# A hybrid convolution block on one core: every pool of 4 KB tiles moved to a multiple of 4 KB in SBUF

## The chip, the core and the metric

The kernel runs on one core of a Trainium2 chip. TensorE (PE, with its weight loads listed as PEld) multiplies, VectorE (DVE) and ScalarE (ACT) work elementwise, GpSimd (POOL) only writes a few constants here, and SyncE (SP) issues nearly all loads and stores. The metric is the device time of one execution in microseconds (us). SBUF is the on-chip memory: 128 partitions, and a tile has the same byte address in each of them. "Remainder" below means a tile's byte address within a partition modulo 4096.

## What is computed

One layer over 256 tokens and 4096 channels, all in float32. The reference, cut to what matters:

```python
c_act = jax.nn.silu(c)
mod = c_act @ w_ada[l] + b_ada[l]                       # 4096 x 12288
shift, scale, gate = jnp.split(mod, 3, axis=-1)
h = _rmsnorm(x, norm_g[l]) * (1.0 + scale[:, None, :]) + shift[:, None, :]
proj = jnp.einsum("bsd,de->bse", h, w_in[l])            # 4096 x 14336
a_b, a_c, a_x, a_z, b_v, b_g, b_z = jnp.split(proj, SPLITS, axis=-1)
y_a = a_b * _causal_depthwise_conv(a_c * a_x, conv_a_w[l]) * jax.nn.silu(a_z)
u = _causal_depthwise_conv(b_v * jax.nn.sigmoid(b_g), conv_b_w[l]) + conv_b_b[l]   # width 31
y_b = jax.nn.silu(_layernorm(u, ln_b_g[l], ln_b_b[l])) * jax.nn.silu(b_z)
x = x + gate[:, None, :] * jnp.einsum("bse,ed->bsd", jnp.concatenate([y_a, y_b], -1), w_out[l])
return _rmsnorm(x, final_g)
```

## The kernel before

**Products.** Each float32 operand is split into a high part (rounded to the format that TensorE multiplies in one pass) and a low rest. `load_w` loads a weight tile of two rows of 128 and 512 columns (512 KB, 4 KB in each partition) into a raw tile `w_r`, ScalarE rounds it to `w_h` (L137), VectorE subtracts to get `w_l` (L138). `products` (L150 to L152) then issues 12 matmuls for the tile: for each of the two rows and the two halves of the tokens, activation-high times `w_h`, activation-high times `w_l`, activation-low times `w_h`. The 512 columns that stream through TensorE (the moving operand, 2 KB in each partition) are always `w_h` or `w_l`; the 128 columns of the activations (`hT` or `yT`, 512 bytes) are loaded as weights before each matmul. There are 576 weight tiles, so 6,912 such matmuls.

**Stages.** The first 448 weight tiles are those of `w_in` (tiles `ps`), taken in six blocks over the 4096 input channels; between them VectorE forms the modulation by dot products over 256 loaded tiles of `w_mod` (L186), and later over 128 tiles of `w_gate`. The width-31 convolution (L347 on ScalarE, L348 on VectorE) is spread over the steps from the last block on. Then come 64 weight tiles of `w_out` for the first half of the channels (tiles `pa`) and 64 for the second half (`pb`). A step is one weight tile; a queue sorted by step numbers says which other work is issued in which step.

**The last 96 matmuls.** The last column tile of `w_out` is done in two passes over the same eight weight tiles: 48 matmuls for the first half of the tokens, then 48 for the second. For the first five of these eight weight tiles (`HOLD = 5`, `keep` in `load_w`) `w_h` and `w_l` lie in the pool `big`, not in the pool `split`. So in each pass 30 matmuls stream out of `big` and then 18 out of `split`; their weights (`yT`) lie in `big` in all of them.

**Pools.** SBUF is filled from address 0 in the order of the pools, and every tile starts at a multiple of 32 bytes. `big` holds 33 tiles of 4 KB (`hT`, `yT`, `acc`, `cv`, `xs` and so on), `cbc` one tile of 16 KB (`cB`, read by L186), `part` four tiles of 16 bytes (running sums of L186), `raws` seven tiles of 4 KB (every raw load), `split` three `w_h` and three `w_l` of 4 KB. The first 16 KB are scratch for DMAs whose descriptors GpSimd writes; this kernel issues none of those. The pools begin at:

| pool | before | remainder | after | remainder |
|---|---|---|---|---|
| `big` | 22,752 | 2,272 | 12,288 | 0 |
| `cbc` | 157,920 | 2,272 | 147,456 | 0 |
| `raws` | 174,432 | 2,400 | 163,840 | 0 |
| `split` | 203,104 | 2,400 | 192,512 | 0 |
| end of `split` | 227,680 | | 217,088 | |

Of the kernel before, what the change touches and what calls it, by code (L numbers as in the profile page):

```python
# [1 line left out]

# [10 lines left out]
F32 = mybir.dt.float32  # L13
# [4 lines left out]
P = 128  # L18
# [65 lines left out]
def decoder_block(ctx: ExitStack, tc: tile.TileContext, x, c, w_mod, w_gate, w_in, w_out, xt, pk, final_g, out):  # L84
    nc = tc.nc
    const = ctx.enter_context(tc.tile_pool(name="const", bufs=1))
    big = ctx.enter_context(tc.tile_pool(name="big", bufs=33))
    cbc = ctx.enter_context(tc.tile_pool(name="cbc", bufs=1))
    part = ctx.enter_context(tc.tile_pool(name="part", bufs=4))
    dram = ctx.enter_context(tc.tile_pool(name="dram", bufs=1, space=bass.MemoryType.DRAM))  # L90
    raws = ctx.enter_context(tc.tile_pool(name="raws", bufs=7))
    split = ctx.enter_context(tc.tile_pool(name="split", bufs=3))
# [6 lines left out]
    def rawt(name, shape=(P, 2, 512)):  # L99
        return raws.tile(list(shape), F32, tag="r", name=name)  # L100
# [59 lines left out]
    modT = const.tile([P, 64], F32, name="modT")  # L160
    gscT = const.tile([P, KT], F32, name="gscT")
    gateT = const.tile([P, KT], F32, name="gateT")
    cB = cbc.tile([P, D], F32, name="cB")
    hT = {}

# [10 lines left out]
    def ada_steps(name, srcs, bias, dst):  # L176

        state = {}

        def step(q):  # L180
            raw = rawt(f"{name}_{q}", (P, ROW))
            nc.sync.dma_start(raw, srcs[q])
            if q == 0:
                state["part"] = part.tile([P, 4], F32, tag="part", name=f"part{name}")
            p = state["part"]
            nc.vector.tensor_tensor_reduce(out=raw, in0=raw, in1=cB[:, q * ROW:(q + 1) * ROW], scale=1.0, scalar=p[:, q - 1:q] if q else bias, op0=ALU.mult, op1=ALU.add, accum_out=dst if q == D // ROW - 1 else p[:, q:q + 1])  # L186

        return [lambda q=q: step(q) for q in range(D // ROW)]
# [431 lines left out]
```

## Time and profile before

| what | value |
|---|---|
| time, median of 3 runs | 1765.87 us (1765.5 to 1768.59) |
| the profiled execution | 1770.85 us, of which its span is 1769.1 us |
| busy: PE, DVE, ACT | 1675.3, 1423.0, 1163.1 us |
| TensorE clock granted over the span | 0.984 of full speed |
| moved by DMA | 524.51 MB, 296 GB/s over the span |

The span runs from the first to the last instruction. Busy times overlap, and matmuls are pipelined: one is on record for about 0.4 us though the next starts some 0.23 us after it. So the pace of TensorE is read from the starts of its matmuls, not from their lengths.

### The profile page before, as it was taken

Reading aid. Unit: us, or ns where it says so; the run is one execution under the profiler, and the core shown is the slowest. Engines: PE = TensorE matmul, PEld = TensorE weight load, DVE = VectorE, ACT = ScalarE, POOL = GpSimd, SP = SyncE. Lnnn points to the kernel's source line nnn. Section 1 sums busy time; section 2 is a strip of 40 time slices with the busy share of each in tenths; the row PEclk is TensorE's granted clock in tenths of the full one; section 3 lists DMA queues with packets and bytes.
Section 4 is the critical chain, followed back from the end, with each engine's and each line's share of the span. In section 5 each row is a group of like instructions: output and inputs, shape, how many; then the busy total and the mean of one; then the engine's idle time right before and its main releaser. Section 6 shows DMA issues by size and latency. Waiting matters only on the chain.

```text
span 1769.1 us, 20848 instructions
## 1 busy us (share of the span) xinstructions
PE 1675.3 (95%) x7073; PEld 1328.7 (75%) x7073; DVE 1423.0 (80%) x1707; ACT 1163.1 (66%) x1558; POOL 1.0 (0%) x8
## 2 busy tenths in 40 slices
PE   4799999999999999999999999989888999999997
PEld 1577788888888888888887787766666777778885
DVE  6877777777777777777776889999999999976665
ACT  4555966566666555565655699898898777464453
POOL 0000000000000000000000000000000000000000
PEclk9899999999999999999999999999999999999998
DMA  8998999999989999999998998868787999678663
GB/s 322 318 367 317 315 325 325 323 320 318 321 312 338 318 313 313 318 330 313 315 320 301 330 317 284 288 225 274 266 266 257 320 313 317 221 272 313 193 199 142
DMA packets 146771, 524.51 MB, mean 296 GB/s; under 512 B 16196, under 2 KB 16228, under 8 KB 146664
## 3 DMA queue, kind: packets, MB, share of 16 engines
q1 hardware_dynamic: 146520, 522.81, 85.3%
q8 instruction: 55, 0.90, 0.2%
q14 instruction: 52, 0.43, 0.1%
q10 hardware_dynamic: 144, 0.37, 0.1%
HBM read 518.91 MB, written 4.21 MB: 296 GB/s over the span
## 4 chain that ended last, share of the span: by engine, by line
PE 66%; DVE 17%; issue 9%; ACT 4%; DMA 4%; DVEq 0%; ACTq 0%
PE ps L151 18%; PE ps L152 17%; PE ps L150 17%; DVE w_l L138 5%; DVE cv L348 5%; DVE gate L186 3%; PE pb L152 3%; PE pb L150 3%; PE pb L151 3%; DMA mod<-in_w_mod 2%; ACT w_h L137 2%; DMA gate<-in_w_gate 1%; ACT pr L347 1%; DVE mod L186 1%; PE pa L151 1%
## 5 line engine op out<-in xcount | busy, mean ns | idle before, releaser
L138 DVE TENSOR_TENSOR w_l<-w_r,w_h 128x1024 fp32r<-128x1024 f32 x576 | 700.5, 1222 | 257.6 <-ACT w_h L137 252.0
L137 ACT CAST w_h<-w_r 128x1024 fp32r<-128x1024 f32 x576 | 598.9, 1045 | 279.0 <-PE ps L152 148.4
L151 PE MATMUL ps<-w_l,hT 128*128 128x512 f32 x1792 | 717.0, 400 | 26.4 <-DVE w_l L138 26.4
L150 PE MATMUL ps<-w_h,hT 128*128 128x512 f32 x1792 | 711.8, 398 | 25.9 <-ACT hT L156 17.8
L152 PE MATMUL ps<-w_h,hT 128*128 128x512 f32 x1792 | 712.3, 398 | 0.8 <-DVE hT L157 0.8
L151 PEld LDWEIGHTS ps<-w_l,hT 128*128 128x128 f32 x1792 | 340.2, 190 | 120.6 <-DVE w_l L138 42.8
L150 PEld LDWEIGHTS ps<-w_h,hT 128*128 128x128 f32 x1792 | 340.4, 190 | 109.9 <-ACT hT L156 18.9
L152 PEld LDWEIGHTS ps<-w_h,hT 128*128 128x128 f32 x1792 | 340.4, 190 | 80.2 <-DVE hT L157 3.0
L443 ACT ACTIVATE acc<-ps 128x1024 f32<-128x1024 f32 x163 | 167.1, 1025 | 234.2 <-PE ps L152 233.9
L186 DVE CUSTOM_DVE_ANT_0 mod<-mod,cB,partmod 128x1024 f32<-128x1024 f32 x192 | 245.6, 1279 | 28.0 <-DMA mod<-in_w_mod 26.3
L347 ACT ACTIVATE pr<-uT,pks 128x255 f32<-128x255 f32 (+14 forms) x480 | 196.9, 487 | 1.1 <-DVE cv L348 1.1
L348 DVE TENSOR_TENSOR cv<-cv,pr 128x1020 f32<-128x1020 f32 (+14 forms) x120 | 138.7, 1156 | 4.5 <-ACT pr L347 4.3
L435 ACT COPY ps<-acc 128x1024 f32<-128x1024 f32 x135 | 137.2, 1017 | 0.4
L186 DVE CUSTOM_DVE_ANT_0 gate<-gate,cB,partgate 128x1024 f32<-128x1024 f32 x96 | 122.8, 1279 | 0.4
L151 PE MATMUL pa<-w_l,yT 128*128 128x512 f32 x256 | 104.6, 409 | 6.3 <-DVE w_l L138 6.1
L150 PE MATMUL pa<-w_h,yT 128*128 128x512 f32 x256 | 101.6, 399 | 1.6 <-ACT w_h L137 1.6
L152 PE MATMUL pa<-w_h,yT 128*128 128x512 f32 x256 | 101.9, 398 | 0.0
L150 PE MATMUL pb<-w_h,yT 128*128 128x512 f32 x256 | 101.0, 394 | 0.0
L152 PE MATMUL pb<-w_h,yT 128*128 128x512 f32 x256 | 100.9, 394 | 0.0
L151 PE MATMUL pb<-w_l,yT 128*128 128x512 f32 x256 | 100.9, 394 | 0.0
L186 DVE CUSTOM_DVE_ANT_0 mod<-mod,cB,pks 128x1024 f32<-128x1024 f32 x64 | 81.9, 1279 | 12.4 <-DMA mod<-in_w_mod 12.4
L151 PEld LDWEIGHTS pa<-w_l,yT 128*128 128x128 f32 x256 | 48.8, 191 | 25.0 <-DVE w_l L138 14.1
(123 smaller groups left out, 676.4 us busy)
## 6 DMA issues: line engine op xcount, KB each, us to landing
w_r<-in_w_in SPq DMA_DIRECT2D x448, 512.0 KB, 5.0
mod<-in_w_mod SPq DMA_DIRECT2D x256, 512.0 KB, 5.2
gate<-in_w_gate SPq DMA_DIRECT2D x128, 512.0 KB, 4.6
w_r<-in_w_out SPq DMA_DIRECT2D x128, 512.0 KB, 4.6
xs<-in_xt SPq DMA_DIRECT2D x8, 512.0 KB, 10.2
xr<-in_x SPq DMA_DIRECT2D x8, 512.0 KB, 6.8
out<-o SPq DMA_DIRECT2D x16, 256.0 KB, 3.0
xc<-in_xt SPq DMA_DIRECT2D x10, 256.0 KB, 4.0
```

The costliest lines, as they stand in the source:

```text
L137: nc.scalar.copy(hi, raw)
L138: nc.vector.tensor_tensor(out=lo, in0=raw, in1=hi.bitcast(F32), op=ALU.subtract)
L150: nc.tensor.matmul(out, ah, hi[:, i], start=f, stop=False, skip_group_check=seeded)
L151: nc.tensor.matmul(out, ah, lo[:, i], start=False, stop=False, skip_group_check=seeded)
L152: nc.tensor.matmul(out, al, hi[:, i], start=False, stop=l, skip_group_check=seeded)
L186: nc.vector.tensor_tensor_reduce(out=raw, in0=raw, in1=cB[:, q * ROW:(q + 1) * ROW], scale=1.0, scalar=p[:, q - 1:q] if q else bias, op0=A ...
L347: nc.scalar.activation(out=pr[:, j, sh:], in_=u[:, j, :S - sh], func=AF.Copy, scale=cbw[:, 4 * i + j, TAPS - 1 - sh:TAPS - sh])
L348: nc.vector.tensor_tensor(out=o[:, :, sh:], in0=o[:, :, sh:], in1=pr[:, :, sh:], op=ALU.add)
L435: nc.scalar.copy(ps, acc[e])
L443: nc.scalar.activation(out=acc[e], in_=ps, func=AF.Silu if k1 == KT and e >= 24 else AF.Copy)
```

## The change

All pools of 4 KB tiles are made to begin at a multiple of 4 KB. The scratch at the front shrinks from 16 KB to 4 KB; a filler tile of 1,680 bytes, which nothing reads or writes, is the first tile of `const`; and the four tiles of running sums move from a pool of their own, which stood ahead of `raws`, into `const`, and are taken in turn by a counter. On each of the five engines the same instructions stand in the same order with the same waits; only the addresses differ (and the names of the running sums).

```diff
+import itertools
...
     const = ctx.enter_context(tc.tile_pool(name="const", bufs=1))
+    const.tile([P, 420], F32, name="pad")
     big = ctx.enter_context(tc.tile_pool(name="big", bufs=33))
     cbc = ctx.enter_context(tc.tile_pool(name="cbc", bufs=1))
-    part = ctx.enter_context(tc.tile_pool(name="part", bufs=4))
...
+    pts = [const.tile([P, 4], F32, name=f"part{i}") for i in range(4)]
+    part_no = itertools.count()
...
             if q == 0:
-                state["part"] = part.tile([P, 4], F32, tag="part", name=f"part{name}")
+                state["part"] = pts[next(part_no) % 4]
...
-    nc = bacc.Bacc("TRN2", target_bir_lowering=False, num_devices=1)
+    nc = bacc.Bacc("TRN2", target_bir_lowering=False, num_devices=1, dynamic_dma_scratch_size=4096)
```

## Rows read from the trace of the kernel before

**Rows 1.** The page: busy times, and slices of the span.

```profile
PE 1675.3 (95%) x7073; PEld 1328.7 (75%) x7073; DVE 1423.0 (80%) x1707; ACT 1163.1 (66%) x1558; POOL 1.0 (0%) x8
...
PE 66%; DVE 17%; issue 9%; ACT 4%; DMA 4%; DVEq 0%; ACTq 0%
```

**Rows 2.** Windows: length, busy PE, PEld, DVE, ACT, POOL (instructions), clock, DMA share, GB/s.

```profile
0.00:60.00 60.00, 24.83 (x46) 13.04 (x47) 43.03 (x64) 23.26 (x25) 0.99 (x8) 0.86 0.86 318
60.00:90.00 30.00, 28.62 (x121) 22.25 (x121) 25.84 (x35) 19.07 (x20) 0.00 (x0) 1.00 0.92 326
90.00:1000.00 910.00, 906.68 (x3888) 730.70 (x3887) 677.82 (x826) 566.08 (x595) 0.00 (x0) 1.00 0.91 320
1000.00:1040.00 40.00, 38.33 (x167) 30.03 (x166) 34.41 (x43) 28.95 (x40) 0.00 (x0) 1.00 0.98 359
1040.00:1560.00 520.00, 480.89 (x2004) 374.02 (x2003) 504.56 (x599) 428.32 (x752) 0.00 (x0) 0.97 0.83 279
1560.00:1740.00 180.00, 179.52 (x785) 145.51 (x784) 125.78 (x114) 89.79 (x116) 0.00 (x0) 1.00 0.68 226
```

**Rows 3.** Timeline of PE: start and length in us; first and last of 174.

```profile
639.77 0.40 PE L152 MATMUL ps<-w_h,hT 128*128 128x512 f32 x1
...
679.97 0.39 PE L151 MATMUL ps<-w_l,hT 128*128 128x512 f32 x1
```

**Rows 4.** The same for the last 96 matmuls, both passes.

```profile
1734.28 0.39 PE L150 MATMUL pb<-w_h,yT 128*128 128x512 f32 x1
...
1735.66 0.39 PE L150 MATMUL pb<-w_h,yT 128*128 128x512 f32 x1
...
1741.10 0.40 PE L150 MATMUL pb<-w_h,yT 128*128 128x512 f32 x1
...
1745.29 0.39 PE L150 MATMUL pb<-w_h,yT 128*128 128x512 f32 x1
1746.67 0.39 PE L150 MATMUL pb<-w_h,yT 128*128 128x512 f32 x1
1752.11 0.40 PE L150 MATMUL pb<-w_h,yT 128*128 128x512 f32 x1
1756.07 0.40 PE L152 MATMUL pb<-w_h,yT 128*128 128x512 f32 x1
```

**Rows 5.** Windows over pieces of those two passes.

```profile
1735.66:1741.10 5.44, 5.44 (x25) 4.51 (x24) 4.00 (x5) 1.34 (x4) 0.00 (x0) 1.00 0.01 2
1741.10:1745.29 4.19, 4.19 (x19) 3.38 (x18) 0.76 (x1) 0.00 (x0) 0.00 (x0) 1.00 0.00 0
1746.67:1752.11 5.44, 5.44 (x26) 4.50 (x24) 3.88 (x14) 4.13 (x7) 0.00 (x0) 1.00 0.10 38
1752.11:1756.07 3.96, 3.96 (x18) 3.19 (x17) 0.15 (x1) 0.03 (x1) 0.00 (x0) 1.00 1.03 381
```

**Rows 6.** Groups of instructions, shapes apart: busy us, mean ns, idle before.

```profile
L138 DVE TENSOR_TENSOR w_l<-w_r,w_h 128x1024 fp32r<-128x1024 f32 x576 | 700.5, 1222 | 257.6 <-ACT w_h L137 252.0 <-DMA w_r<-in_w_out 3.1 <-DMA xr<-in_x 1.6
L186 DVE CUSTOM_DVE_ANT_0 mod<-mod,cB,partmod 128x1024 f32<-128x1024 f32 x192 | 245.6, 1279 | 28.0 <-DMA mod<-in_w_mod 26.3 <-ACT cB L174 0.6 <-DVE w_l L138 0.3
L186 DVE DVE_READ_ACCUMULATOR2_ANT partmod<- 128x1 f32 x192 | 15.8, 83 | 0.0
L507 DVE TENSOR_TENSOR o<-o,xr 128x1024 f32<-128x1024 f32 x7 | 8.6, 1225 | 0.2
L157 DVE TENSOR_TENSOR hT<-xc,hT 128x512 fp32r<-128x512 f32 x10 | 6.9, 686 | 0.2 <-ACT hT L156 0.2
```

**Rows 7.** The page: a costly group, and DMA issues (KB each, us to landing).

```profile
L348 DVE TENSOR_TENSOR cv<-cv,pr 128x1020 f32<-128x1020 f32 (+14 forms) x120 | 138.7, 1156 | 4.5 <-ACT pr L347 4.3
...
w_r<-in_w_in SPq DMA_DIRECT2D x448, 512.0 KB, 5.0
...
fg<-in_final_g SPq DMA_DIRECT2D x4, 512.0 KB, 5.0
```

## Prediction

> **What bounds the kernel now.** I began with the page: TensorE is busy for 95% of the span, and PE has 66% of the chain that ended last [rows 1]. The windows by stage then say where that holds [rows 2]. From 90 to 1000 us TensorE is busy for 906.68 of 910 us and from 1560 to 1740 for 179.52 of 180, while VectorE and ScalarE have room; there the pace of the matmuls is the pace of the kernel. From 1040 to 1560 us VectorE is busy for 504.56 of 520 us and TensorE for 480.89: there VectorE sets the pace. The first 60 us belong to loads and to VectorE.
>
> The third view is the timeline of TensorE, read for the distance between starts. In a dense stretch 174 matmuls start from 639.77 to 679.97 us: 40.20 / 173 = 232.4 ns for each [rows 3]. Nothing else waits there, so this is TensorE's own pace.
>
> The last 96 matmuls are a test that the kernel makes by itself [rows 4]. They have the same form, one pass after another over the same tiles; only the pool of the moving operand changes. I leave out the first weight tile of each pass, where the pace is still changing. The next 24 matmuls, which stream out of `big`, take 1741.10 - 1735.66 = 5.44 us, or 226.7 ns each. The 18 after them, out of `split`, take 1745.29 - 1741.10 = 4.19 us, or 232.8 ns. In the second pass it is the same: 1752.11 - 1746.67 = 5.44 us for 24, 226.7 ns; 1756.07 - 1752.11 = 3.96 us for 17 intervals, 232.9 ns. Could other work explain it? In the first pass the slow piece is the quiet one, with VectorE at 0.76 us and no DMA, and the fast piece has VectorE busy for 4.00 us; in the second pass the slow piece runs beside DMA at a share of 1.03 and keeps the same pace [rows 5]. So neither engines nor DMA set it. What is left is where the moving operand lies: its remainder is 2,272 (or 224 for the second row) in `big` and 2,400 (or 352) in `split`, while the weights lie in `big`, 2,272 plus multiples of 512, in both.
>
> **The change, part by part.** No instruction, wait or queue entry is added, removed or moved, so all that can change is how long something takes at its new address.
>
> *Matmuls.* After the change the moving operand starts at remainder 0 or 2,048 and the weights at multiples of 512. Relative to each other they then stand as they do in the fast piece: equal modulo 512. I take the pace of that piece, 226.7 ns, for all matmuls: 232.4 - 226.7 = 5.7 ns each. It counts where TensorE sets the pace: 906.68 us / 0.2324 = 3,901 matmuls from 90 to 1000 us, and (1734.28 - 1560) / 0.2324 = 750 from 1560 us to the last passes [rows 2 to 4]. 4,651 x 5.7 ns = 26.5 us.
>
> From 60 to 90 and from 1000 to 1040 us TensorE is busy for 28.62 + 38.33 = 66.95 us, 288 matmuls, worth up to 1.6 us; loads are close to their limit there (DMA share 0.92 and 0.98), so I take 0.8, with 0 and 1.6 as ends. From 1040 to 1560 us a faster TensorE only waits longer for VectorE. At most VectorE's own idle time, 520 - 504.56 = 15.4 us, could go; at worst the longer waits let the clock, 0.97 now, fall in more places. Should it be 0.94, another 0.03 x 520 = 15.6 us of granted clock is lost, of which VectorE's pace hides most. I take a gain of 1 us, with -8 and +11.8 (2,069 matmuls x 5.7 ns) as ends.
>
> The loads must keep up. From 90 to 1000 us they run at 320 GB/s at a share of 0.91, so about 352 GB/s would be full; a pace of 226.7 ns asks for 320 x 232.4 / 226.7 = 328 GB/s, and 359 were moved from 1000 to 1040 us [rows 2]. That is enough on the mean. VectorE's 677.82 us of work and ScalarE's 566.08 fit into 888 us.
>
> *VectorE and ScalarE.* The two inputs of L138 have the same remainder now (2,400), and so do those of L507 (2,272): 1222 and 1225 ns [rows 6]. L348 reads its tiles from a start that moves in steps of 4 bytes from tap to tap, and its mean is 1156 ns at a mean of 962 columns (4 x (256 - 15.5)); the slope from L157 to L138, (1222 - 686) / 512 = 1.05 ns a column, gives 1222 - 62 x 1.05 = 1157 [rows 6, 7]. By these rows the time on VectorE does not depend on where a tile starts. Only L186 reads two remainders at once (2,400 and 2,272) and will read equal ones; no row has it otherwise. The 3 ns between L138 and L507 bound it at 384 x 3 ns = 1.2 us either way; I take 0.
>
> *Running sums.* They keep their size, order and waits; the 83 ns read-out that follows [rows 6] stays as it is. Nothing. If a wait were to come up, it would stand on VectorE ahead of L138, for which the matmuls L151 wait. *Scratch:* no DMA uses it. Nothing. *Loads:* a load into `raws` (remainder 2,400) lands after 5.0 us, and one into `big` (2,272) as well [rows 7], so I take 0; the first 60 us, at a DMA share of 0.86, could give a little, and I put 1 us either way.
>
> *Sum.* 26.5 + 0.8 + 1 = 28.3 us. The profiled execution took 1770.85 us, so 1742.5 for its like; the median of the runs lies 5 us lower, at 1765.87, and from there it is **1738 us**. A change of 0.2%, 3.5 us, is about what a measurement of this kernel can tell from none.
>
> By the Trainium skill this sum would be nothing: "SBUF — State Buffer", Specifications (TRN2), has SBUF in lines of 16 bytes, with a penalty for accesses that cross to a new line. 2,272 and 2,400, and the 0 of after, are all multiples of 16, so by that rule `big` and `split` should go equally fast now; the two paces above don't agree with that.
>
> **The rivals.**
>
> *Only the place counts, not the remainder.* The fast tiles lie below 157,920 and the slow ones above 203,104; perhaps that alone is the difference, and remainders don't matter. After the change `split` lies at 192,512 to 217,088, mostly where it is slow now. Speaks for it: the trace has just the two pools, so it cannot tell them apart. Against it: L138 reads `raws` and writes `split` at the time of L507, which stays in `big`. Time: 1766, no change. If the border lies between the new tiles, some of the `w_h` gain, a third to all of them; two of three matmuls read `w_h`, so 2/9 to 2/3 of 28 us, 1760 to 1747. I give it 15% for no change and 4% for a part.
>
> *Clean starts do better than the fast piece.* If the remainder itself counts and 0 is the best, 226.7 ns is not the floor: 512 columns, one a cycle of the full clock (2.4 GHz), are 213.3 ns. At that bound 4,651 x 19.1 = 89 us would go; but then 320 GB/s would become 349, all that 352 allow, and loads would hold part of it back. Between 1690 and 1730; 16%. The skill's page "TensorE: Matmul & The Clock Gate", section "Wait — 56ns, not 53.3ns?", gives the columns' time plus about 2.5 ns, here 215.8 ns; my estimate from it is 77 us, thus 1689. No matmul of this form in the trace runs at that.
>
> *Loads can't follow.* TensorE takes on the faster pace, but the seven tiles of `raws` don't come round in time, and waits for loads from 90 to 1000 us give back a third to nine tenths of the gain. For it: the share of 0.91 is an average. Against it: TensorE idles there for only 3.3 of 910 us. 1746 to 1760; 8%.
>
> *Equal starts collide: slower.* After the change the moving operand, the weights, and what VectorE and ScalarE read and write all begin at the same low addresses. If reads of the weights then meet reads of the moving operand, the pace rises above 232.4 ns. It decides from 233.2 ns on (0.75 ns x 4,651 = 3.5 us); at 240 ns it would be 7.6 x 4,651 = 35 us, 1801. Against it: in `big` both have equal starts modulo 512 already, and that is the fast piece. 7%.
>
> **The numbers.** The forecast has 50%: 1738, with 1730 to 1747 as its own range by the ends above. Faster: 50 + 16 + 8 + 4 = 78%; same: 15%; slower: 7%. For the range, 1705 cuts off a third of the second rival (5%), and 1767 cuts off the slower case (7%) and the upper part of no change (6%): 18% outside.
>
> **What would show it.** In a dense stretch from 90 to 1000 us matmuls should start 226.7 ns apart, and in the last passes the pieces out of `big` and out of `split` should have one pace. The stretch that is 910 us now should take 888, and the one from 1040 to 1560 should keep its length with TensorE less busy. L138, L186 and L137 should keep their means within 5 ns. I am wrong if the two pieces of the last passes still differ by 6 ns (place), if the pace is 226.7 but TensorE waits for loads, or if the dense pace is above 232.4.

## The result, and the profile after

The changed kernel takes 1744.09 us (median of 4 runs, 1741.25 to 1744.85) beside 1767.23 us for the kernel before on the same chip: a ratio of 0.9863, 95% interval 0.9841 to 0.9885. So it is 1.4% faster. In the profiles the span fell from 1769.1 to 1743.0 us. Most lines of the changed code stand three further down, those of `products` and `load_w` one: L150 to L152 are L151 to L153 there, L138 is L139; L186 is L189.

The pace comes first. This is the timeline of TensorE in the changed kernel, start and length in us: the first and the last of 179 matmuls of a dense stretch, the place of [rows 3].

```profile
639.62 0.39 PE L153 MATMUL ps<-w_h,hT 128*128 128x512 f32 x1
...
679.97 0.39 PE L151 MATMUL ps<-w_h,hT 128*128 128x512 f32 x1
```

(679.97 - 639.62) / 178 = 226.7 ns from start to start, where it was 232.4. The last two passes of the changed kernel, the places of [rows 4]:

```profile
1710.20 0.39 PE L151 MATMUL pb<-w_h,yT 128*128 128x512 f32 x1
1715.64 0.39 PE L151 MATMUL pb<-w_h,yT 128*128 128x512 f32 x1
1719.72 0.39 PE L151 MATMUL pb<-w_h,yT 128*128 128x512 f32 x1
1721.08 0.39 PE L151 MATMUL pb<-w_h,yT 128*128 128x512 f32 x1
1726.52 0.39 PE L151 MATMUL pb<-w_h,yT 128*128 128x512 f32 x1
1730.38 0.39 PE L153 MATMUL pb<-w_h,yT 128*128 128x512 f32 x1
```

The 24 matmuls out of `big` take 1715.64 - 1710.20 = 5.44 us, as before, and the 18 out of `split` take 1719.72 - 1715.64 = 4.08 us: both 226.7 ns. In the second pass it is 5.44 us again, and 3.86 us for 17 intervals, 227 ns. The step between the two pools is gone.

Where was the time won? In each kernel I take the start of the first matmul of step 0, of step 20, of step 320, of step 500, and that of the last matmul. A step is 12 matmuls, so the count between two of them is known. First the timeline of the kernel before (its last row is the end of [rows 4], 1756.07):

```profile
52.94 0.80 PE L150 MATMUL ps<-w_h,hT 128*128 128x512 f32 x1 [16.74 <-ACT hT L156]
114.26 0.39 PE L150 MATMUL ps<-w_h,hT 128*128 128x512 f32 x1
955.30 0.39 PE L150 MATMUL ps<-w_h,hT 128*128 128x512 f32 x1
1531.47 0.40 PE L150 MATMUL pa<-w_h,yT 128*128 128x512 f32 x1
```

and of the changed kernel (its last row is 1730.38, above):

```profile
53.78 0.79 PE L151 MATMUL ps<-w_h,hT 128*128 128x512 f32 x1 [16.74 <-ACT hT L157]
114.96 0.39 PE L151 MATMUL ps<-w_h,hT 128*128 128x512 f32 x1
935.98 0.39 PE L151 MATMUL ps<-w_h,hT 128*128 128x512 f32 x1
1509.89 0.39 PE L151 MATMUL pa<-w_h,yT 128*128 128x512 f32 x1
```

One profile of each kernel doesn't show what belongs to a single execution. So the same marks (step 20, step 320, step 500, the last matmul) follow for a second pair, both described below: `e2_scratch_only`, which has the addresses of before 12,288 bytes lower, then `a2_whole_again`, the changed kernel once more.

```profile
114.57 0.40 PE L150 MATMUL ps<-w_h,hT 128*128 128x512 f32 x1
954.85 0.39 PE L150 MATMUL ps<-w_h,hT 128*128 128x512 f32 x1
1525.96 0.40 PE L150 MATMUL pa<-w_h,yT 128*128 128x512 f32 x1
1749.43 0.40 PE L152 MATMUL pb<-w_h,yT 128*128 128x512 f32 x1
...
113.11 0.39 PE L151 MATMUL ps<-w_h,hT 128*128 128x512 f32 x1
933.87 0.39 PE L151 MATMUL ps<-w_h,hT 128*128 128x512 f32 x1
1506.20 0.39 PE L151 MATMUL pa<-w_h,yT 128*128 128x512 f32 x1
1726.69 0.39 PE L153 MATMUL pb<-w_h,yT 128*128 128x512 f32 x1
```

| stretch | matmuls | before, us | after, us | won, us | won, second pair, us | 5.7 ns each, us |
|---|---|---|---|---|---|---|
| up to step 20 | 240 | 114.26 | 114.96 | -0.7 | 1.5 | |
| step 20 to 320 | 3,600 | 841.04 | 821.02 | 20.0 | 19.5 | 20.5 |
| step 320 to 500 | 2,160 | 576.17 | 573.91 | 2.3 | -1.2 | 12.3 |
| step 500 to the last matmul | 911 | 224.60 | 220.49 | 4.1 | 3.0 | 4.9 |

In the last row 60 of the 911 matmuls stream out of `big` and had nothing to win, so 5.7 ns are counted for 851. With 0.3 us after the last matmul the first pair makes the 26.0 us between the two profiled executions (1770.85 and 1744.85), the second its 23.1 us (1764.19 and 1741.13). Where TensorE sets the pace, nearly every matmul from step 20 to 320 hands on its 5.7 ns, and most do after step 500. In the middle stretch, where VectorE sets it, a gain can't be told from none: 2.3 us in one pair, -1.2 in the other. What the matmuls save there goes into waiting: the intervals of 300 ns and more from start to start, without the matmuls at the lower clock (427 ns), add up to 96.2 us there in the trace of before and to 107.7 after, and to 95.2 and 107.7 in the second pair. The windows of the changed kernel (length, busy PE, PEld, DVE, ACT, POOL with instructions, clock, DMA share, GB/s) show the same beside [rows 2]:

```profile
90.00:1000.00 910.00, 903.83 (x3958) 742.32 (x3957) 694.72 (x849) 578.45 (x611) 0.00 (x0) 1.00 0.93 328
1020.00:1535.00 515.00, 473.31 (x1998) 369.69 (x1997) 503.54 (x598) 426.65 (x748) 0.00 (x0) 0.97 0.83 280
```

Loads keep up at 328 GB/s in place of 320. In the stretch that VectorE sets, it is busy for 503.54 of 515 us, beside 504.56 of 520, and the granted clock is 0.97 as before.

Groups of the changed kernel, the counterparts of [rows 6, 7] (busy us, mean ns, idle before):

```profile
L139 DVE TENSOR_TENSOR w_l<-w_r,w_h 128x1024 fp32r<-128x1024 f32 x576 | 702.7, 1226 | 236.1 <-ACT w_h L138 234.3 <-PE ps L152 0.6
L189 DVE CUSTOM_DVE_ANT_0 mod<-mod,cB,part 128x1024 f32<-128x1024 f32 x192 | 245.7, 1280 | 26.0 <-DMA mod<-in_w_mod 24.1 <-ACT cB L177 1.4
L189 DVE CUSTOM_DVE_ANT_0 gate<-gate,cB,part 128x1024 f32<-128x1024 f32 x96 | 124.2, 1294 | 1.6 <-DMA gate<-in_w_gate 1.5
...
w_r<-in_w_in SPq DMA_DIRECT2D x448, 512.0 KB, 5.0
...
L351 DVE TENSOR_TENSOR cv<-cv,pr 128x1020 f32<-128x1020 f32 (+14 forms) x120 | 140.3, 1169 | 3.6 <-ACT pr L350 3.4
```

The means are those of before within 4 ns, but for the gate's dot products (1294) and L351 (1169). The second profile of the same kernel, `a2_whole_again`, has 1278 and 1155 there, so this belongs to one execution and not to the addresses.

### The profile page after: what moved, and what is told of

Its sections match the earlier page's. It is cut to its first block, busy times and chain, and to the rows that moved or that the text cites. A ratio compares the mean times of both kernels' runs of the same rounds, so it can differ in the third digit from the quotient of the medians.

```text
span 1743.0 us, 20848 instructions
## 1 busy us (share of the span) xinstructions
PE 1644.6 (94%) x7073; PEld 1323.9 (76%) x7073; DVE 1421.8 (82%) x1707; ACT 1163.6 (67%) x1558; POOL 1.0 (0%) x8
## 4 chain that ended last, share of the span: by engine, by line
PE 63%; DVE 18%; issue 10%; ACT 5%; DMA 4%; DVEq 0%; ACTq 0%
PE ps L152 17%; PE ps L153 17%; PE ps L151 17%; DVE w_l L139 5%; DVE cv L351 5%; DVE gate L189 3%; PE pb L151 3%; PE pb L153 3%; PE pb L152 3%; DMA mod<-in_w_mod 2%; ACT w_h L138 2%; ACT pr L350 1%; DVE mod L189 1%; DMA gate<-in_w_gate 1%; PE cps L176 1%
## 5 line engine op out<-in xcount | busy, mean ns | idle before, releaser
L139 DVE TENSOR_TENSOR w_l<-w_r,w_h 128x1024 fp32r<-128x1024 f32 x576 | 702.7, 1226 | 236.1 <-ACT w_h L138 234.3
L138 ACT CAST w_h<-w_r 128x1024 fp32r<-128x1024 f32 x576 | 600.2, 1048 | 260.1 <-PE ps L153 140.7
L152 PE MATMUL ps<-w_l,hT 128*128 128x512 f32 x1792 | 709.4, 396 | 26.5 <-DVE w_l L139 26.3
L151 PE MATMUL ps<-w_h,hT 128*128 128x512 f32 x1792 | 703.4, 393 | 27.6 <-ACT hT L157 18.1
L153 PE MATMUL ps<-w_h,hT 128*128 128x512 f32 x1792 | 703.6, 393 | 1.1 <-DVE hT L158 1.1
L152 PEld LDWEIGHTS ps<-w_l,hT 128*128 128x128 f32 x1792 | 339.2, 189 | 115.4 <-DVE w_l L139 46.2
L151 PEld LDWEIGHTS ps<-w_h,hT 128*128 128x128 f32 x1792 | 339.5, 190 | 104.0 <-ACT hT L157 19.2
L153 PEld LDWEIGHTS ps<-w_h,hT 128*128 128x128 f32 x1792 | 339.6, 190 | 71.9 <-DVE hT L158 3.2
L189 DVE CUSTOM_DVE_ANT_0 mod<-mod,cB,part 128x1024 f32<-128x1024 f32 x192 | 245.7, 1280 | 26.0 <-DMA mod<-in_w_mod 24.1
L351 DVE TENSOR_TENSOR cv<-cv,pr 128x1020 f32<-128x1020 f32 (+14 forms) x120 | 140.3, 1169 | 3.6 <-ACT pr L350 3.4
L189 DVE CUSTOM_DVE_ANT_0 gate<-gate,cB,part 128x1024 f32<-128x1024 f32 x96 | 124.2, 1294 | 1.6 <-DMA gate<-in_w_gate 1.5
L152 PE MATMUL pa<-w_l,yT 128*128 128x512 f32 x256 | 104.0, 406 | 7.9 <-DVE w_l L139 7.4
L151 PE MATMUL pa<-w_h,yT 128*128 128x512 f32 x256 | 100.3, 394 | 1.8 <-ACT w_h L138 1.8
L153 PE MATMUL pa<-w_h,yT 128*128 128x512 f32 x256 | 100.9, 394 | 0.0
L151 PE MATMUL pb<-w_h,yT 128*128 128x512 f32 x256 | 99.7, 389 | 0.0
L152 PE MATMUL pb<-w_l,yT 128*128 128x512 f32 x256 | 99.6, 389 | 0.0
L153 PE MATMUL pb<-w_h,yT 128*128 128x512 f32 x256 | 99.6, 389 | 0.0
L189 DVE CUSTOM_DVE_ANT_0 mod<-mod,cB,pks 128x1024 f32<-128x1024 f32 x64 | 81.9, 1280 | 12.3 <-DMA mod<-in_w_mod 12.3
L152 PEld LDWEIGHTS pa<-w_l,yT 128*128 128x128 f32 x256 | 48.7, 190 | 27.4 <-DVE w_l L139 17.6
```

The lines of the kernel that those rows point to most:

```text
L138: nc.scalar.copy(hi, raw)
L139: nc.vector.tensor_tensor(out=lo, in0=raw, in1=hi.bitcast(F32), op=ALU.subtract)
L151: nc.tensor.matmul(out, ah, hi[:, i], start=f, stop=False, skip_group_check=seeded)
L152: nc.tensor.matmul(out, ah, lo[:, i], start=False, stop=False, skip_group_check=seeded)
L153: nc.tensor.matmul(out, al, hi[:, i], start=False, stop=l, skip_group_check=seeded)
L351: nc.vector.tensor_tensor(out=o[:, :, sh:], in0=o[:, :, sh:], in1=pr[:, :, sh:], op=ALU.add)
```

## The experiments

The theory at this point: TensorE's pace depends on the distance between the start of the moving operand (`w_h` or `w_l`, in `split`) and that of the weights (`hT` or `yT`, in `big`), modulo some power of two. The two rivals are that the moving operand's own remainder counts, and that its place in SBUF does. The trace of before couldn't tell them apart.

### One part alone: the running sums

```diff
+import itertools
...
-    part = ctx.enter_context(tc.tile_pool(name="part", bufs=4))
...
+    pts = [const.tile([P, 4], F32, name=f"part{i}") for i in range(4)]
+    part_no = itertools.count()
...
-                state["part"] = part.tile([P, 4], F32, tag="part", name=f"part{name}")
+                state["part"] = pts[next(part_no) % 4]
```

> The kernel before with one part of the change: the running sums move into the constants. No filler, scratch as before. The pool of the split weight tiles stays at 203,104 (remainder 2,400); big moves by 128 bytes to 22,880, so that every pool has remainder 2,400 and moving operand and weights are equal modulo 512. Theory 'relative' (the distance between moving operand and weights modulo 512 counts): dense pace 226.7 ns, the last passes with one pace, ratio 0.986 as for the whole change (about 1743 us). Theory 'own remainder' (the moving operand's own start counts, and 0 is a good one, 2,400 a bad one): 232.4 ns, no change (ratio 1.000). Theory 'place' (where split lies in SBUF): its address is the same, so 232.4 ns and no change.

Measured: 1745.41 us, a ratio of 0.988 (0.9864 to 0.9895). The timeline of TensorE, first and last of 179 in a dense stretch, then the same places of the second of the last passes:

```profile
639.61 0.39 PE L152 MATMUL ps<-w_l,hT 128*128 128x512 f32 x1
...
679.96 0.39 PE L153 MATMUL ps<-w_h,hT 128*128 128x512 f32 x1
...
1727.08 0.39 PE L151 MATMUL pb<-w_h,yT 128*128 128x512 f32 x1
1730.93 0.39 PE L153 MATMUL pb<-w_h,yT 128*128 128x512 f32 x1
```

40.35 / 178 = 226.7 ns, and 3.85 / 17 = 226.5 ns out of `split`. `split` has not moved by a byte; `big` moved by 128 bytes and no pool begins at a multiple of 4 KB. Both rivals fall by this run alone. A third, that the weights' own remainder counts, is left by it, as `big` has moved; it falls by the last passes of before, where the same weights have two paces [rows 4], and by `e3_apart_128` below. The ratio 0.988 is a little above the 0.9863 of the whole change; whether that is a difference is asked at the end of this section.

### One part alone: the scratch

```diff
-    nc = bacc.Bacc("TRN2", target_bir_lowering=False, num_devices=1)
+    nc = bacc.Bacc("TRN2", target_bir_lowering=False, num_devices=1, dynamic_dma_scratch_size=4096)
```

> The kernel before with one part of the change: scratch 4 KB in place of 16 KB. All pools lie 12,288 bytes lower, with the remainders of before (2,272 and 2,400); split lies at 190,816 to 215,392, close to where it lies after the whole change. Relative: the moving operand is 128 bytes off the weights, 232.4 ns, ratio 1.000. Own remainder: the same, 1.000. Place: faster, up to the whole gain, ratio 0.986 to 0.997.

Measured: 1770.65 us, a ratio of 1.0017 (1.0004 to 1.0031): no gain. The interval lies just above 1, by 0.04 to 0.31%; none of the three theories has such a loss, and the profiled execution, 1764.19 us, is the fastest of the ten, so its trace doesn't show where it comes from. The timeline, first and last of 174:

```profile
639.74 0.39 PE L150 MATMUL ps<-w_h,hT 128*128 128x512 f32 x1
...
679.94 0.39 PE L152 MATMUL ps<-w_h,hT 128*128 128x512 f32 x1
```

40.20 / 173 = 232.4 ns, with `split` 12,288 bytes lower. The place doesn't count.

### The whole change, and 128 bytes

The edit to the changed kernel:

```diff
+    gap = ctx.enter_context(tc.tile_pool(name="gap", bufs=1))
+    gap.tile([P, 32], F32, name="gap_pad")
     raws = ctx.enter_context(tc.tile_pool(name="raws", bufs=7))
```

> The whole change, with 128 bytes of filler ahead of raws: big at remainder 0, raws and split at remainder 128. Relative: 128 bytes apart again, so the gain is gone: dense pace 232.4 ns, about 1766 us, ratio 1.000, though big is still at multiples of 4 KB. Own remainder: the moving operand starts at 128 modulo 512, a start that no run has had; between 226.7 and 233 ns. Place: as after the change, ratio 0.986.

Measured: 1768.82 us, a ratio of 1.0003 (0.9989 to 1.0016). The timeline, first and last of 173, and the second of the last passes from its 24 matmuls out of `big` on:

```profile
639.81 0.40 PE L153 MATMUL ps<-w_h,hT 128*128 128x512 f32 x1
...
679.77 0.39 PE L154 MATMUL ps<-w_l,hT 128*128 128x512 f32 x1
...
1743.04 0.39 PE L153 MATMUL pb<-w_h,yT 128*128 128x512 f32 x1
1748.48 0.40 PE L153 MATMUL pb<-w_h,yT 128*128 128x512 f32 x1
1752.44 0.40 PE L155 MATMUL pb<-w_h,yT 128*128 128x512 f32 x1
```

39.96 / 172 = 232.3 ns, and the two paces of the last passes are back: 5.44 us for 24 (226.7 ns), 3.96 us for 17 (232.9 ns). 128 bytes undo the whole gain, with `big`, where 33 of the 46 tiles of 4 KB lie, still at multiples of 4 KB.

### Other distances

In three more kernels the three pairs of split tiles, taken in turn, lie at three remainders, so that each step of 12 matmuls has one distance. `big`, `cbc` and `raws` stay at 0. The edit of the first one to the changed kernel:

```diff
-    split = ctx.enter_context(tc.tile_pool(name="split", bufs=3))
+    splits, at = [], 0
+    for j, off in enumerate((32, 64, 256)):
+        if off > at:
+            gap = ctx.enter_context(tc.tile_pool(name=f"gap{j}", bufs=1))
+            gap.tile([P, (off - at) // 4], F32, name=f"gap_pad{j}")
+        splits.append(ctx.enter_context(tc.tile_pool(name=f"split{j}", bufs=1)))
+        at = off
+    split_no = itertools.count()
...
+            split = splits[next(split_no) % 3]
```

> The whole change, but the three pairs of split tiles, which are used in turn, lie at remainders 32, 64 and 256 in place of 0; a step of 12 matmuls has one of them. Relative: a pace by step, with 226.7 ns only where the distance is a multiple of what counts; from the two paces seen, 0 and 128 apart, 64 and 32 should be at or above 226.7 and 256 tells whether the period is shorter than 512. Own remainder: the same steps, no other forecast, since big lies at 0. If only a multiple of 128 other than 0 costs something, all three could run at 226.7 ns.

One run: 1759.49 us, with 1768.01 us as the median of before on that chip. Its timeline: the first and the last of the 12 matmuls of three steps in a row, at distances 32, 64 and 256.

```profile
644.22 0.40 PE L159 MATMUL ps<-w_h,hT 128*128 128x512 f32 x1
...
646.79 0.40 PE L161 MATMUL ps<-w_h,hT 128*128 128x512 f32 x1
647.03 0.40 PE L159 MATMUL ps<-w_h,hT 128*128 128x512 f32 x1
...
649.55 0.39 PE L161 MATMUL ps<-w_h,hT 128*128 128x512 f32 x1
649.78 0.39 PE L159 MATMUL ps<-w_h,hT 128*128 128x512 f32 x1
...
652.30 0.39 PE L161 MATMUL ps<-w_h,hT 128*128 128x512 f32 x1
```

2.57, 2.52 and 2.52 us for 11 intervals: 233.6, 229 and 229 ns. The pace changes from step to step with the tile that is read. The three distances come in turn through the whole trace, so that other work meets all of them alike.

> The whole change, but the three pairs of split tiles at remainders 96, 160 and 192, used in turn. The runs so far give, by distance between moving operand and weights: 0: 226.7, 32: 233.6, 64: 229.0, 128: 232.5, 256: 227.1 ns. Theory 'the distance counts modulo 256, the same on both sides': 192 as 64 (229), 96 and 160 alike, at 229 to 234 ns. Theory 'the distance counts, but only its size up to the length of the weights (512 bytes)': 160 and 192 between 232.5 and 227, falling. None below 226.7 by either; if a distance gives less, it is the start of a better layout.

> The whole change, but the three pairs of split tiles at remainders 224, 288 and 384, used in turn. Theory 'modulo 256': 288 as 32 (233.6 ns), 384 as 128 (232.5 ns), 224 as 32 if both sides are alike. Theory 'the size of the distance up to 512': 288 and 384 close to the 227.1 ns of 256.

One run of each: 1772.42 and 1772.84 us, beside a single 1771.9 for before; the readings below rest on the traces, not on these times. The table has the mean from start to start over all steps of a distance in each of these traces (intervals of 300 ns and more left out: waits, and matmuls at the lower clock), and for 0 and 128 that of the changed kernel and of `e3_apart_128`.

| distance, bytes | 0 | 32 | 64 | 96 | 128 | 160 | 192 | 224 | 256 | 288 | 384 |
|---|---|---|---|---|---|---|---|---|---|---|---|
| mean, ns | 227.3 | 233.6 | 229.9 | 233.2 | 232.5 | 233.9 | 233.1 | 233.3 | 229.2 | 233.4 | 233.1 |
| intervals | 6,640 | 2,213 | 2,200 | 2,211 | 6,608 | 2,210 | 2,200 | 2,211 | 2,196 | 2,205 | 2,190 |

The pace of a step settles only after some matmuls when the step ahead had another distance. In the last six intervals of their steps, 256 has 227.4 ns and 64 has 229.0; the others don't fall. So 256 is as good as 0, 288 goes as 32, 384 as 128: the theory "modulo 256" holds in the three pairs that were measured (320, the partner of 64, was not), and "only the size up to 512" falls. `s2_96_160_192` refutes a part of my expectation, that both sides are alike: 192 costs 233.1 ns and not what 64 costs. No distance gives less than 0 does.

### Do multiples of 4 KB give something of their own?

The changed kernel and the one with the running sums alone, on one chip.

> The changed kernel once more, on the same chip as the next one. Theory 'only the distance between moving operand and weights counts': ratio 0.986 to 0.988, and the same as the next kernel within 0.1%. Theory 'multiples of 4 KB give something of their own': 0.2% or more below the next kernel.

> The kernel with the running sums alone moved, every pool at remainder 2,400. Only the distance: ratio 0.986 to 0.988, as the changed kernel. Multiples of 4 KB of their own: 0.988 to 0.990 beside 0.986 for the changed kernel.

Measured: 1743.14 us, ratio 0.9862 (0.9842 to 0.9882), and 1742.72 us, ratio 0.9854 (0.9838 to 0.987). The two can't be told apart, though 0.9854 lies just below the 0.986 to 0.988 that was expected. The filler and the smaller scratch bring nothing that can be measured; neither is needed.

## Why the prediction was right

**The pace.** Forecast 226.7 ns, measured 226.7 ns, taken from the 24 matmuls that happened to have equal starts already. The reading that the distance modulo 512 counts was right in kind; the sweep shows that the period is 256 bytes. That the distance is the cause is shown by `e1_sums_only` and `e3_apart_128`, which set it apart from the remainder and the place by 128 bytes each way.

**The sum.** The large term, 26.5 us for 4,651 matmuls at TensorE's own pace, is over by a little: the stretches from step 20 to 320 and from step 500 to the end, 4,451 matmuls that had something to win, gave 20.0 + 4.1 = 24.1 of 25.4 us, and 19.5 + 3.0 = 22.5 in the second pair. The term for the stretch that VectorE sets, with 1 us between -8 and +11.8, was 2.3 and -1.2 us from step 320 to 500, loads near their limit at its start included: nothing that can be told from 0 or from 1. The start, where I had put 0 with 1 us either way, gave -0.7 and 1.5 us. The first pair of profiles gives 26.0 us of 28.3, and that it comes so close is in part luck: the profiled execution of before lies 3.6 us above its median, that of after 0.8 above. The second pair gives 23.1 us and the medians 1767.23 - 1744.09 = 23.1. So the sum is over by some 2 to 5 us; where the rest went isn't shown. 1744 us lies 6 us above the forecast, 1.4 of them because the median of before is 1767.23 with a fourth run, and within the forecast's own range.

Two bounds of the prediction are slips that change nothing here. A gain of 11.8 us in place of 1 takes 1738 to 1727, not to 1730; and with nine tenths of the gain given back "Loads can't follow" ends at 1763, not at 1760.

**The clock.** The fear that longer waits cost clock did not come true: the granted clock was 0.97 in that stretch before and after. From step 320 to 500 the four traces with equal starts have 36 to 45 matmuls at the lower clock, and those of before, `e2_scratch_only` and `e3_apart_128` 30 to 45.

**The rivals.** "Only the place counts" is refuted by `e1_sums_only` and `e2_scratch_only`. "Clean starts do better" is refuted: at remainder 0 the pace is 226.7 ns, as at 2,400 with equal starts. "Loads can't follow" happened only in small: of the 20.5 us due from step 20 to 320, 20.0 and 19.5 came. "Equal starts collide" is refuted; unequal ones are the slower.

**VectorE, ScalarE, loads, running sums.** Nothing, as forecast: the means of all runs are alike but for the one execution named above, and loads of weight tiles into `raws` land after 5.0 to 5.1 us at either remainder.

What stays open is what in the chip makes the distance count; that the reads of the two operands disturb each other isn't shown. All weights here are equal modulo 256, so the runs don't say whether it is the weights of the running matmul or those being loaded for the next one that count. One thing the traces do show: at the lower of TensorE's two clocks (1.2 GHz, half of 2.4) the distance costs nothing. Here are windows at a granted clock of 0.50 about step 504, in the kernel before and in the changed one, each with the first and the last matmul in it.

```profile
1550.32:1554.59 4.27, 4.27 (x12) 3.30 (x10) 4.24 (x6) 0.73 (x1) 0.00 (x0) 0.50 1.00 391
1550.32 0.63 PE L152 MATMUL pa<-w_h,yT 128*128 128x512 f32 x1
...
1554.59 0.63 PE L150 MATMUL pa<-w_h,yT 128*128 128x512 f32 x1
...
1528.95:1532.79 3.84, 3.84 (x10) 2.97 (x9) 3.81 (x6) 0.67 (x1) 0.00 (x0) 0.50 1.02 406
1528.95 0.63 PE L153 MATMUL pa<-w_h,yT 128*128 128x512 f32 x1
...
1532.79 0.63 PE L153 MATMUL pa<-w_h,yT 128*128 128x512 f32 x1
```

4.27 / 10 = 427 ns at 128 bytes apart and 3.84 / 9 = 426.7 ns at equal starts; the three kernels with other distances have a mean of 426.7 ns at that clock too. That is the time of 512 cycles at 1.2 GHz, 426.7 ns. At 2.4 GHz as many cycles are 213.3 ns; the pace at equal starts is 13 ns above that and the pace at 128 bytes apart 19 ns, and no run here shows what these are.

## What to carry to other kernels

When the same matmul goes at two paces in one trace, compare the addresses of its operands before you look for a wait: a quiet piece that is slower than a busy one cannot be explained by other work. For matmuls of this form (512 moving columns and 128 columns of weights in float32, at the full clock) put the moving operand and the weights at equal starts modulo 256 bytes; other forms weren't measured. Here a pool of 16-byte tiles between two large pools had set them 128 bytes apart, which cost 5 to 6 ns on nearly all of the 6,912 matmuls. It paid where TensorE set the pace, and a gain of 1.2 to 1.5% was to be had by moving 128 bytes of tiles, with no alignment to 4 KB.

## What was not expected of the hardware

A distance of 64 bytes costs less than the others (229.0 ns settled, beside 232.5 to 233.9), but 192 does not. At half the clock the distance costs nothing: 427 ns from start to start in both kernels. And the pace has a memory: after a step with another distance, the steps at 256 bytes begin at 230 to 235 ns in their first five intervals and settle at 227 after them.
